# A one-layer attention block: x loaded through other queues, tiles of x and weights by turns in the first chunk, and the norm's squares from a second load of x by rows

## The chip, the cores and the metric

The kernel runs on one core of a Trainium2 chip. The metric is the device time of one execution in microseconds (us); lower is better. The engines are PE (TensorE, matrix products), ACT (ScalarE), DVE (VectorE), POOL (GpSimd) and SP (SyncE, which here only issues transfers). ACT, POOL and SP can issue transfers (DMAs) as well; each engine works through its own instructions in their order, and an instruction that waits holds up all behind it.

## The reference

The input x has 512 tokens of 4096 features. With one layer, the block is:

```
h   = x * rsqrt(mean(x*x) + eps) * norm_g          # RMS norm over the features
q, k, v, z = split(h @ w_in + b_in)                # 4096 x 9216 weights
o   = attention(q, k, v)                           # causal window of 128 keys, sinks
x   = x + (o * z * sigmoid(z)) @ w_out + b_out     # 4096 x 4096 weights
out = x * rsqrt(mean(x*x) + eps) * final_g
```

All arrays are float32.

## The kernel before

**Precision.** A float32 operand is split into a high part in PE's format and a low remainder. ACT makes the high part, DVE the low one, and each product is three matmuls: high by high, high by low, low by high.

**Input projection.** The contraction over 4096 features runs in `NC` = 8 chunks `kc` of `KC` = 4 tiles of 128 features. The columns of `w_in` form 72 tiles `t` of 128. One *slot* (kc, t) is 4 feature tiles by 3 matmuls, so 12 matmuls of 128x128 by 128x512. Weights of a slot are 256 KB; `load_w` (L151) brings them through SP's queue into one of `RAW` = 3 buffers, and `split_w` (L160) splits them into `whi` (ACT, L128) and `wlo` (DVE, L129), with `WB` = 4 buffers of each.

**The stage that matters here** comes first: while x arrives, the first `NPRE` = 4 column tiles run chunk by chunk (L492), 8 chunks by 4 slots, 32 slots in all. Later column tiles find all of x split in SBUF.

**Loading x** (`load_x`, L186). x comes transposed, feature by token. A transfer of 512 KB brings two feature tiles (`xraw`, two buffers, so one chunk); the first chunk takes four of 256 KB. All of them go through SP's queue, among the weights. Of each tile ACT makes `xh` (L199, with the norm's gain), DVE `xl` (L200). For the norm, tiles are squared (`xq`; the first four on POOL, L209, the others on ACT, L207), and POOL adds all squares up (L213). The gain's factor per token (`norm_column`, L229) follows behind slot (7, 1): PE sums the squares over the features in 8 small matmuls (`pv`), then DVE and ACT take the inverse root, and PE spreads it to a row behind slot (7, 2).

**What sets the order.** PE runs in the order of the text. A scheduler orders the other engines when the program is built; `tc.issue_after` sets an instruction behind another. Ahead of the first load lie `WARM` = 9 matmuls on zeros.

**Later work.** Attention of each group of heads runs behind later slots, its output goes to DRAM through POOL's queue (L465); then follow the output projection, residual and final norm (`scale_out`, `land`, `bring`).

Of the kernel before, what the change touches and what calls it, by code (L numbers as in the profile page):

```python
# [8 lines left out]
F32 = mybir.dt.float32  # L9
# [21 lines left out]
NCC = D // CW  # L31
EPS = 1e-5
# [9 lines left out]
def hybrid_block_kernel(  # L42
# [25 lines left out]
    # 1 where the key lies in the query's own block (key <= query); queries of two heads on the rows  # L68
# [10 lines left out]
    nc.scalar.activation(ones[:, 2:], ones[:, 2:], AF.Exp)  # L79
# [15 lines left out]
    # The tensor engine runs in the order of this text.  # L95
# [6 lines left out]
    # Work that is due behind a later slot of the projections' matmuls.  # L102
# [29 lines left out]
    def rsqrt(v, y, n):  # L132
        """y = v ** -0.5, one Newton step behind the table's root."""
        a = small.tile([P, n], F32, name="rs_a", tag="rs_a", bufs=2)
        nc.scalar.activation(a, v, AF.Sqrt)
        nc.vector.reciprocal(y, a)
        nc.vector.tensor_tensor(a, y, y, op=ALU.mult)
        nc.vector.tensor_tensor(a, a, v, op=ALU.mult)
        nc.vector.tensor_scalar(a, a, -0.5, 1.5, op0=ALU.mult, op1=ALU.add)
        nc.vector.tensor_tensor(y, y, a, op=ALU.mult)  # L140

    # Work beside the weights' stream takes its turn behind the latest of its loads and splits.
# [8 lines left out]
    def load_w(src, half=None):  # L151
        """Two tiles of weights, or one; split as they are needed."""
        raw = wpool.tile([P, 2, CW], F32, name="raw", tag="raw", bufs=RAW)
        if half is None:
            latest[0] = nc.sync.dma_start(raw, src.rearrange("p (j c) -> p j c", j=2))
        else:
            latest[0] = nc.sync.dma_start(raw[:, half], src)  # L157
        return raw
# [8 lines left out]
    with ExitStack() as ph:  # L167
# [5 lines left out]
        # the tensor engine's clock is let up by work alone: run it on zeros until the first loads land  # L173
# [10 lines left out]
        squares = [None]  # L184

        def load_x(kc, whole=True):  # L186
            xh[kc] = xg.tile([P, KC, S], F32R, name=f"xh{kc}", tag="hi", bufs=NC)
            xl[kc] = xg.tile([P, KC, S], F32R, name=f"xl{kc}", tag="lo", bufs=NC)
            for i in range(KC // 2):
                raw = att.tile([P, 2, S], F32, name="xraw", tag="q2", bufs=2)  # L190
                src = xT[kc * KC // 2 + i].rearrange("p (j s) -> p j s", j=2)
                if whole:
                    nc.sync.dma_start(raw, src)
                for j in range(2):
                    if not whole:
                        nc.sync.dma_start(raw[:, j], src[:, j])
                    kt = kc * KC + 2 * i + j
                    h, l = xh[kc][:, 2 * i + j, :], xl[kc][:, 2 * i + j, :]
                    high = nc.scalar.activation(h, raw[:, j], AF.Copy, scale=gcol[:, kt:kt + 1])  # L199
                    nc.vector.scalar_tensor_tensor(  # L200
                        l, raw[:, j], gcol[:, kt:kt + 1], h.bitcast(F32),
                        op0=ALU.mult, op1=ALU.subtract,
                    )
                    q = att.tile([P, S], F32, name="xq", tag="tmp" if kt else "z", bufs=2 if kt else 1)
                    with tc.issue_after(high.ins):
                        if whole:
                            nc.scalar.activation(q, raw[:, j], AF.Square)  # L207
                        else:
                            nc.gpsimd.tensor_tensor(q, raw[:, j], raw[:, j], op=ALU.mult)  # L209
                    if kt == 0:  # L210
                        squares[0] = q
                    else:
                        nc.gpsimd.tensor_tensor(squares[0], squares[0], q, op=ALU.add)  # L213

        def mm_chunk(acc, kc, raw):
            wh, wl = split_w(raw, kc % 2)
            for j in range(KC):
                h, l = wh[:, j * P:(j + 1) * P], wl[:, j * P:(j + 1) * P]
                xhj, xlj = xh[kc][:, j, :], xl[kc][:, j, :]
                mm(acc, h, xhj, start=(kc == 0 and j == 0), stop=False)  # L220
                mm(acc, h, xlj, start=False, stop=False)
                mm(acc, l, xhj, start=False, stop=(kc == NC - 1 and j == KC - 1))
# [6 lines left out]
        def norm_column():  # L229
            """rsqrt(mean(x[t]**2) + EPS), a block of tokens in a column."""  # L230
            pv = ps_t.tile([P, NB, 2], F32, name="pv", tag="pt")
            for b in range(NB):
                mm(pv[:, b], squares[0][:, b * P:(b + 1) * P], ones[:, 0:2], start=True, stop=True)
            v = small.tile([P, NB], F32, name="v4")
            nc.vector.tensor_scalar(v, pv[:, :, 0], 1.0 / D, EPS, op0=ALU.mult, op1=ALU.add)
            r = small.tile([P, NB], F32, name="r4")
            rsqrt(v, r, NB)
            return r

        def norm_row(r):  # L240
# [14 lines left out]
        def kv_tile(g, acc):  # L255
# [12 lines left out]
            # vv[:, m]: the values of the 128 keys from 64 (m - 1) on; vw[:, m]: those of the 64 keys  # L268
            # from 64 m on, twice
# [23 lines left out]
        def q_tile(g, p, acc):  # L293
# [12 lines left out]
            # the high parts of both pairs of a four, one above the other  # L306
# [58 lines left out]
        def turn(n, pr):  # L365
            """The weights by key, split in two: the window's first 128 keys, and the 64 that follow."""
# [40 lines left out]
        def quad(g, i, q2, qh, kh, vv, vw):  # L407
            """The attention of a group's heads 4i to 4i + 3."""
# [31 lines left out]
        def gate(g, p, acc):  # L440
            """z / (1 + exp(-z))."""
# [48 lines left out]
        NPRE = 4  # L490
        accs = [ps_m.tile([P, S], F32, name="acc") for _ in range(NPRE)]
        for kc, t in ((kc, t) for kc in range(NC) for t in range(NPRE)):  # L492
            k2, i = divmod(kc, 2)
            raw = load_w(w_in[t, k2, :, i * CW:(i + 1) * CW], half=i)
            if t == 0 == kc:
                with tc.issue_after(latest[0].ins):
                    nc.sync.dma_start(gcol, norm_g)
                    load_x(kc, False)
            if t == 1 and kc < NC - 1:
                with tc.issue_after(latest[0].ins):  # L500
                    load_x(kc + 1)
            mm_chunk(accs[t], kc, raw)
            if kc == NC - 1:
                if t == 1:
                    r = norm_column()
                elif t == 2:
                    norm_row(r)
                for i in {2: (0, 1, 2), 3: (3,)}.get(t, ()):
                    evacuate(i, accs[i])
        for t in range(NPRE, NT):  # L510
            acc = ps_m.tile([P, S], F32, name="acc")
            for kc in range(NC):
                if kc % 2 == 0:
                    raw = load_w(w_in[t, kc // 2])
                mm_chunk(acc, kc, raw)
                if t == NT - 1 and kc:
                    behind(lambda: load_g(kc - 1))
                if t == NT - 1 and kc == NC - 1:
                    evacuate(t, acc)
                tick()  # L520
# [50 lines left out]
    def scale_out(tb, fg, xb):  # L571
        """The final norm of a block's rows, a chunk of columns at a time; the last has its gains to come."""
# [37 lines left out]
    for cc in range(NCC):  # L610
# [6 lines left out]
        for kt in range(HOLD, KT) if last else ():  # L617
            # the last weights stay, so that the blocks end one after the other
# [18 lines left out]
def _columns():  # L637
    """The projection's columns by key-value head: k and v, then queries and gates, two heads at a time."""
# [45 lines left out]
```

## Time and profile before

| | |
|---|---|
| time, median of 3 runs | 2437.08 us (2435.55 to 2439.21) |
| profiled execution, its span | 2435.7 us, 1.4 us below the median; no time of its own is listed apart |
| PE busy | 2406.7 us, 99% of the span |
| DVE, ACT, POOL busy | 1436.5, 992.8, 362.2 us |
| DMA | 266.31 MB, 109 GB/s over the span |

The first of the profile's 40 slices are the stage in which x arrives: PE is busy for 8 tenths of the first slice, and 9 or more in the next ones, where matmuls at half clock count as busy too. So the busy share alone hides what is lost; the timeline, with start times of single matmuls, shows it. The granted clock (PEclk) is 1.00 at 2.4 GHz and 0.50 at 1.2 GHz.

### The profile page before, as it was taken

What the parts mean: (1) busy time and instruction counts of PE and PEld (TensorE: products, weight loads), DVE (VectorE), ACT (ScalarE), POOL (GpSimd) and SP (SyncE); (2) the same over time, 40 slices, a digit from 0 to 9 for tenths busy, and PEclk for the clock granted to TensorE, in tenths of its full rate; (3) what the DMA queues carried; (4) which work ended last, traced back from release to release, by engine and by line L of the source; (5) the groups of instructions that cost most, each with busy time, mean ns of one, the idle gap of its engine ahead of it and who ended that gap; (6) DMA issues with size and microseconds to landing.
All of it is one profiled execution on the core that took longest, in us unless ns stands there. A gap on an engine that the chain in (4) does not pass through costs nothing.

```text
span 2435.7 us, 30364 instructions
## 1 busy us (share of the span) xinstructions
PE 2406.7 (99%) x11033; PEld 1999.4 (82%) x11033; DVE 1436.5 (59%) x2513; ACT 992.8 (41%) x2142; POOL 362.2 (15%) x459
## 2 busy tenths in 40 slices
PE   8899999999999999999999999999999999999997
PEld 6688888888888888888888888888888888888886
DVE  7576465646646464564655556465765664665565
ACT  5454343333434333342433334343444444444444
POOL 6221110201111020110101011010210110110110
PEclk9999999999999999999999999999999999999999
DMA  5323323323232333223233232323733432343335
GB/s 188 124 88 95 104 91 91 102 90 102 85 104 87 100 96 96 95 91 100 91 93 101 88 102 85 103 88 102 261 117 102 127 122 95 121 123 99 125 117 182
DMA packets 80550, 266.31 MB, mean 109 GB/s; under 512 B 9440, under 2 KB 9472, under 8 KB 80400
## 3 DMA queue, kind: packets, MB, share of 16 engines
q1 hardware_dynamic: 73904, 243.32, 32.4%
q0 software_dynamic: 6496, 21.05, 2.6%
q8 instruction: 87, 1.43, 0.2%
q14 instruction: 63, 0.52, 0.1%
HBM read 247.55 MB, written 16.78 MB: 109 GB/s over the span
## 4 chain that ended last, share of the span: by engine, by line
PE 97%; DVE 1%; DMA 1%; issue 1%; ACT 0%; POOL 0%; SPq 0%; DVEq 0%; POOLq 0%
PE acc L97 92%; PE ps L97 2%; PE po L97 2%; PE pt L100 1%; DMA xraw<-in_xT 1%; DVE xl L200 0%; DVE wlo L129 0%; PE pv L100 0%; ACT xh L199 0%; DVE y L586 0%; ACT xq L207 0%; ACT whi L128 0%; POOL wl L379 0%; SPq L157 0%; POOL wh L379 0%
## 5 line engine op out<-in xcount | busy, mean ns | idle before, releaser
L129 DVE TENSOR_TENSOR wlo<-raw,whi 128x512 fp32r<-128x512 f32 x822 | 596.0, 727 | 758.7 <-ACT whi L128 749.1
L128 ACT CAST whi<-raw 128x512 fp32r<-128x512 f32 x822 | 510.9, 622 | 1208.1 <-PE acc L97 1154.0
L97 PE MATMUL acc<-xh,wlo 128*128 128x512 f32 x2304 | 901.4, 391 | 11.7 <-DVE wlo L129 11.6
L97 PE MATMUL acc<-xh,whi 128*128 128x512 f32 x2304 | 904.7, 393 | 2.4 <-ACT xh L199 1.9
L97 PE MATMUL acc<-xl,whi 128*128 128x512 f32 x2304 | 900.9, 391 | 0.6 <-DVE xl L200 0.4
L97 PE MATMUL acc<-whi,gs 128*128 128x512 f32 x1968 | 606.3, 389 | 0.0
L97 PEld LDWEIGHTS acc<-xh,wlo 128*128 128x128 f32 x2304 | 433.9, 188 | 107.4 <-DVE wlo L129 15.5
L97 PEld LDWEIGHTS acc<-xh,whi 128*128 128x128 f32 x2304 | 434.5, 189 | 89.2 <-ACT xh L199 2.8
L97 PEld LDWEIGHTS acc<-xl,whi 128*128 128x128 f32 x2304 | 434.3, 188 | 87.8 <-DVE xl L200 2.9
L97 PEld LDWEIGHTS acc<-whi,gs 128*128 128x128 f32 x1968 | 369.6, 188 | 76.4
L97 PE MATMUL acc<-wlo,gs 128*128 128x512 f32 x984 | 383.2, 389 | 0.0
L97 PEld LDWEIGHTS acc<-wlo,gs 128*128 128x128 f32 x984 | 184.8, 188 | 38.2
L129 DVE TENSOR_TENSOR gs<-g,gs 128x512 fp32r<-128x512 f32 x256 | 191.2, 788 | 0.6 <-ACT gs L128 0.6
L379 POOL TENSOR_SCALAR_AFFINE_SELECT ww<-wh 64x512 fp32r<-64x512 f32 x64 | 42.1, 658 | 830.6 <-ACT wh L375 830.6
L128 ACT CAST gs<-g 128x512 fp32r<-128x512 f32 x256 | 145.8, 617 | 1.7 <-PE acc L97 1.7
L353 ACT ACTIVATE prob<-ps,nm 128x128 f32<-128x128 f32 x256 | 90.3, 365 | 78.6 <-DVE nm L344 75.0
L451 DVE RECIPROCAL e<-e 128x128 f32<-128x128 f32 x128 | 120.7, 945 | 0.5
L598 POOL DMA_DIRECT2D xb<-in_x x32 | 17.3, 540 | 502.3 <-DVE y L608 502.3
L428 ACT COPY ot<-po 64x256 f32<-64x256 f32 x128 | 47.0, 367 | 55.6 <-DVE o L429 40.1
L429 DVE TENSOR_TENSOR o<-po,ot 64x256 f32<-64x256 f32 x128 | 52.8, 412 | 20.3 <-ACT ot L428 19.8
L302 DVE SCALAR_TENSOR_TENSOR q<-tmp,bcol,q 64x512 fp32r<-64x512 f32 x64 | 59.4, 927 | 6.6 <-ACT q L301 5.4
L226 DVE TENSOR_TENSOR tmp<-acc,rbc 128x512 f32<-128x512 f32 x41 | 28.4, 692 | 57.2 <-PE acc L97 56.7
(111 smaller groups left out, 1501.6 us busy)
## 6 DMA issues: line engine op xcount, KB each, us to landing
raw<-in_w_in SPq DMA_DIRECT2D x272, 512.0 KB, 3.6
raw<-in_w_out SPq DMA_DIRECT2D x128, 512.0 KB, 3.6
raw<-in_w_in SPq DMA_DIRECT2D x32, 256.0 KB, 3.2
gT<-o POOLq DMA_DIRECT2D x32, 256.0 KB, 2.3
g<-gT SPq DMA_DIRECT2D x16, 512.0 KB, 7.0
xb<-in_x POOLq DMA_DIRECT2D x32, 256.0 KB, 3.6
out_y<-y SPq DMA_DIRECT2D x32, 256.0 KB, 3.0
xraw<-in_xT SPq DMA_DIRECT2D x14, 512.0 KB, 4.2
```

The source lines that it names most:

```text
L97: tc.keep_in_program_order(nc.tensor.matmul(*a, **k))
L100: tc.keep_in_program_order(nc.tensor.transpose(*a, **k))
L128: nc.scalar.copy(hi, src),
L129: nc.vector.tensor_tensor(lo, src, hi.bitcast(F32), op=ALU.subtract),
L226: nc.vector.tensor_tensor(t, acc, rbc, op=ALU.mult)
L302: nc.vector.scalar_tensor_tensor(q2[other, :, h, :], tv[own], b[own], q2[own, :, h, :].bitcast(F32), op0=ALU.add, op1=ALU.subtract,)
L353: nc.scalar.activation(pr[:, u, a, :], ps[:, u, a, 0:P], AF.Exp, bias=nm[:, u, a:a + 1], scale=SCALE, accum_out=den[:, u, a:a + 1],)
L379: nc.gpsimd.affine_select(out=out, in_=src.bitcast(F32), fill=0.0, pattern=[[0, 8], [1 if own else -1, QH]], compare_op=ALU.is_ge if own e ...
L428: nc.scalar.copy(ot[own], pq[other, :, :, h, :])
L429: nc.vector.tensor_tensor(ov[own], pq[own, :, :, h, :], ot[own], op=ALU.add)
L451: nc.vector.reciprocal(c, c)
L598: nc.gpsimd.dma_start(xb, x[tb * P:(tb + 1) * P, cs])
```

## The change

1. **Queues.** The four transfers of x's first chunk are issued by ACT, the fourteen of 512 KB by POOL; SP carries weights and the gains alone. Staging takes four buffers by turns (tags `q2`, `o`, `q2`, `qq`), so two chunks.
2. **Order.** `x_tile` splits one tile of x behind the weights' split of a slot, one per slot and one chunk ahead. In chunk 0, tile m of x and weights of column tile m come by turns, and PE takes the products as both exist (3, then 9, 15 and 21 matmuls) instead of slot by slot.
3. **Squares.** `xq` and POOL's sums are gone. Instead `x_row` loads x again by rows, token by feature, in 16 pieces of 128 tokens by 1024 features (512 KB), through POOL's queue into two buffers (tags `vv`, `vw`), and ACT squares each with a sum into a column of `sums`. `norm_column` adds four columns on DVE; the 8 matmuls `pv` are gone.
4. The first ACT function (`Exp` on `ones`, with its table) is placed behind the first issues. Comments and docstrings are gone too; they are left out below.

```diff
+RC = 4
...
-        def load_x(kc, whole=True):
+        STAGE = ("q2", "o", "q2", "qq")
+        def load_x(kc):
...
             for i in range(KC // 2):
-                raw = att.tile([P, 2, S], F32, name="xraw", tag="q2", bufs=2)
-                if whole:
-                    nc.sync.dma_start(raw, src)
+                k2 = kc * KC // 2 + i
+                tag = STAGE[k2 % len(STAGE)]
+                raw = att.tile([P, 2, S], F32, name="xraw", tag=tag, bufs=2 if tag == "q2" else 1)
+                if kc:
+                    nc.gpsimd.dma_start(raw, src)
                 for j in range(2):
-                    if not whole:
-                        nc.sync.dma_start(raw[:, j], src[:, j])
...
-                    q = att.tile([P, S], F32, name="xq", tag="tmp" if kt else "z", bufs=2 if kt else 1)
-                    with tc.issue_after(high.ins):
-                        if whole:
-                            nc.scalar.activation(q, raw[:, j], AF.Square)
-                        else:
-                            nc.gpsimd.tensor_tensor(q, raw[:, j], raw[:, j], op=ALU.mult)
-                    if kt == 0:
-                        squares[0] = q
-                    else:
-                        nc.gpsimd.tensor_tensor(squares[0], squares[0], q, op=ALU.add)
+                    if not kc:
+                        nc.scalar.dma_start(raw[:, j], src[:, j])
+                    landed[2 * k2 + j] = raw[:, j]
+        def x_tile(kt):
+            kc, j = divmod(kt, KC)
+            raw = landed.pop(kt)
+            h, l = xh[kc][:, j, :], xl[kc][:, j, :]
+            high = nc.scalar.activation(h, raw, AF.Copy, scale=gcol[:, kt:kt + 1])
+            low = nc.vector.scalar_tensor_tensor(
+                l, raw, gcol[:, kt:kt + 1], h.bitcast(F32), op0=ALU.mult, op1=ALU.subtract
+            )
+            return high, low
+        def x_row(i):
+            tb, c = divmod(i, RC)
+            w = D // RC
...
+            nc.gpsimd.dma_start(raw, x[tb * P:(tb + 1) * P, c * w:(c + 1) * w])
+            nc.scalar.activation(raw, raw, AF.Square, accum_out=sums[:, tb, c:c + 1])
...
-            pv = ps_t.tile([P, NB, 2], F32, name="pv", tag="pt")
-            for b in range(NB):
-                mm(pv[:, b], squares[0][:, b * P:(b + 1) * P], ones[:, 0:2], start=True, stop=True)
-            nc.vector.tensor_scalar(v, pv[:, :, 0], 1.0 / D, EPS, op0=ALU.mult, op1=ALU.add)
+            nc.vector.tensor_reduce(v, sums, axis=AX.X, op=ALU.add)
+            nc.vector.tensor_scalar(v, v, 1.0 / D, EPS, op0=ALU.mult, op1=ALU.add)
...
+        load_x(0)
+        raws = [load_w(w_in[0, 0, :, 0:CW], half=0)]
+        nc.sync.dma_start(gcol, norm_g)
+        nc.scalar.activation(ones[:, 2:], ones[:, 2:], AF.Exp)
+        raws += [load_w(w_in[m, 0, :, 0:CW], half=0) for m in range(1, RAW)]
+        load_x(1)
+        for m in range(NPRE):
+            if m == RAW:
+                raws.append(load_w(w_in[m, 0, :, 0:CW], half=0))
+            first.append(after(last, split_w, raws[m], 0))
+            last = after(latest[1:], x_tile, m)
+            for t, j in [(m, j) for j in range(m)] + [(t, m) for t in range(m + 1)]:
+                mm_tile(accs[t], 0, j, *first[t])
+        for j in range(KC):
+            last = after(last, x_tile, KC + j)
+        for kc, t in ((kc, t) for kc in range(1, NC) for t in range(NPRE)):
...
+            w = split_w(raw, i)
+            if kc < NC - 1:
+                if t == 0:
+                    load_x(kc + 1)
+                last = after(latest[1:], x_tile, (kc + 1) * KC + t)
+            if ROW0 <= kc * NPRE + t < ROW0 + NB * RC:
+                after(latest[1:], x_row, kc * NPRE + t - ROW0)
+            mm_chunk(accs[t], kc, w)
```

Where the instructions come to stand (names: `raw` weights, `xraw` x transposed, `row` x by rows; xN is a count of equal instructions in a row):

SP's queue from the start of the program, before:

```order
L157 DMA raw<-in_w_in 128x512
L497 DMA gcol<-in_norm_g 128x32
L196 DMA xraw<-in_xT 128x512 x4
L157 DMA raw<-in_w_in 128x512 x3
L193 DMA xraw<-in_xT 128x1024
L157 DMA raw<-in_w_in 128x512 x3
L193 DMA xraw<-in_xT 128x1024
```

and from its end of the stage, before:

```order
L193 DMA xraw<-in_xT 128x1024 x2
L157 DMA raw<-in_w_in 128x512 x4
L193 DMA xraw<-in_xT 128x1024 x2
L157 DMA raw<-in_w_in 128x512 x6
```

The same queue over the whole stage, now:

```order
L157 DMA raw<-in_w_in 128x512
L516 DMA gcol<-in_norm_g 128x32
L157 DMA raw<-in_w_in 128x512 x31
```

No transfer of x stands behind a weight load any more, and none of the weights behind one of x.

ACT while the tiles of chunk 5 are split (`xh_567`), before:

```order
L199 ACTIVATE xh_567<-xraw,gcol 128x512
L128 CAST whi<-raw 128x512
L207 ACTIVATE xq<-xraw 128x512
L199 ACTIVATE xh_567<-xraw,gcol 128x512
L207 ACTIVATE xq<-xraw 128x512
L199 ACTIVATE xh_567<-xraw,gcol 128x512 x2
L128 CAST whi<-raw 128x512
L207 ACTIVATE xq<-xraw 128x512 x2
L128 CAST whi<-raw 128x512 x2
```

and now (`xh_519`):

```order
L211 ACTIVATE xh_519<-xraw,gcol 128x512
L227 ACTIVATE row,sums<-row 128x1024 x2
L128 CAST whi<-raw 128x512
L211 ACTIVATE xh_519<-xraw,gcol 128x512
L128 CAST whi<-raw 128x512
L211 ACTIVATE xh_519<-xraw,gcol 128x512
L227 ACTIVATE row,sums<-row 128x1024
L128 CAST whi<-raw 128x512
L211 ACTIVATE xh_519<-xraw,gcol 128x512
L227 ACTIVATE row,sums<-row 128x1024
```

The splits of x and of the weights now alternate, and squares of rows stand between them; a `whi` behind a square waits for that square's transfer.

POOL behind its constants, before:

```order
L209 TENSOR_TENSOR xq<-xraw 128x512 x3
L213 TENSOR_TENSOR xq<-xq 128x512 x2
L209 TENSOR_TENSOR xq<-xraw 128x512
L213 TENSOR_TENSOR xq<-xq 128x512 x29
```

and now, the first rows and the last:

```order
L200 DMA xraw<-in_xT 128x1024 x2
L226 DMA row<-in_x 128x1024 x2
L200 DMA xraw<-in_xT 128x1024 x6
L226 DMA row<-in_x 128x1024
L200 DMA xraw<-in_xT 128x1024
L226 DMA row<-in_x 128x1024
```

```order
L200 DMA xraw<-in_xT 128x1024
L226 DMA row<-in_x 128x1024
L200 DMA xraw<-in_xT 128x1024
L226 DMA row<-in_x 128x1024 x6
```

POOL computes nothing in this stage any more; it issues 14 transfers of x and 16 of rows in one order, each waiting for its buffer. Behind this stage the instructions of every engine stand in the same order as before.

## Rows read from the trace of the kernel before

**Rows 1.** The page: span, and the engines' shares of the chain that ended last.

```profile
span 2435.7 us, 30364 instructions
...
PE 97%; DVE 1%; DMA 1%; issue 1%; ACT 0%; POOL 0%; SPq 0%; DVEq 0%; POOLq 0%
```

**Rows 2.** Waits of PE from 112 us to the end: total us, times, longest.

```profile
PE po L97 <- POOL wl L379: 0.4, 1, 0.4
```

**Rows 3.** Timeline of PE: start us, us, engine, line, operation, out<-in, count, idle before.

```profile
6.17 0.51 PE L97 MATMUL acc<-xh,whi 128*128 128x512 f32 x1 [1.31 <-ACT xh L199]
...
9.90 0.63 PE L97 MATMUL acc<-xh,wlo 128*128 128x512 f32 x1
10.33 0.63 PE L97 MATMUL acc<-xh,whi 128*128 128x512 f32 x1
...
22.17 0.39 PE L97 MATMUL acc<-xh,whi 128*128 128x512 f32 x1
...
111.46 0.95 PE L97 MATMUL pv<-ones,xq 128*128 128x2 f32 x8
112.27 0.48 PE L97 MATMUL acc<-xh,whi 128*128 128x512 f32 x1
```

**Rows 4.** Stretches: bounds, length, busy us (count) by engine, PEclk, DMA share, GB/s.

```profile
22.17:42.80 20.63, 20.13 (x87) 15.77 (x85) 17.75 (x16) 15.00 (x26) 15.31 (x10) 1.00 0.65 205
42.80:111.62 68.82, 57.11 (x229) 44.33 (x229) 40.11 (x39) 29.86 (x53) 23.12 (x16) 0.95 0.46 147
```

**Rows 5.** Timeline of ACT behind the last x tile.

```profile
108.71 0.62 ACT L128 CAST whi<-raw 128x512 fp32r<-128x512 f32 x1 [2.10 <-PE acc L97]
111.43 0.62 ACT L128 CAST whi<-raw 128x512 fp32r<-128x512 f32 x1 [2.10 <-PE acc L97]
```

**Rows 6.** Waits of SP's queue from 0 to 112 us, then timelines of SP and ACT.

```profile
SPq L157 <- DVE wlo L129: 63.7, 25, 9.4
...
54.36 12.87 SPq L157 DMA_DIRECT2D raw<-in_w_in  x4
67.28 2.73 SPq L193 DMA_DIRECT2D xraw<-in_xT  x2
...
73.00 0.72 ACT L199 ACTIVATE xh<-xraw,gcol 128x512 fp32r<-128x512 f32 x1 [8.91 <-DMA xraw<-in_xT]
```

**Rows 7.** Groups and operations up to 115 us: count, ns as mean or min/median/max.

```profile
L213 POOL TENSOR_TENSOR xq<-xq 128x512 f32<-128x512 f32 x31 | 46.6, 1505 | 38.8 <-ACT xq L207 37.6
L199 ACT ACTIVATE xh<-xraw,gcol x32: 705/716/726, 5.4 to 92.6; 128x512 fp32r<-128x512 f32 x32
L200 DVE SCALAR_TENSOR_TENSOR xl<-xraw,gcol,xh x32: 739/1463/1804, 6.2 to 95.7; 128x512 fp32r<-128x512 f32 x32
L128 ACT CAST whi<-raw x34: 601/611/625, 3.7 to 111.4; 128x512 fp32r<-128x512 f32 x34
L129 DVE TENSOR_TENSOR wlo<-raw,whi x33: 676/692/1780, 4.9 to 109.4; 128x512 fp32r<-128x512 f32 x33
```

**Rows 8.** Stretches of 2 us, columns as in rows 4.

```profile
2.00:4.00 2.00, 2.00 (x6) 0.76 (x5) 0.40 (x1) 0.57 (x3) 1.82 (x6) 1.00 0.77 235
4.00:6.00 2.00, 0.86 (x4) 0.11 (x1) 0.80 (x2) 0.94 (x2) 0.74 (x2) 1.00 0.80 212
6.00:8.00 2.00, 1.25 (x3) 0.48 (x3) 0.89 (x1) 0.49 (x2) 0.82 (x2) 0.92 0.95 302
```

**Rows 9.** Squares of the last stage, DMA issues of POOL, and landing of x tiles and xb.

```profile
L606 ACT ACTIVATE y<-xb x32: 613/627/634, 1812.6 to 2423.9; 128x512 f32<-128x512 f32 x32
L606 ACT ACTIVATION_READ_ACCUMULATOR y<-xb x32: 183/186/189, 1813.1 to 2424.5; 128x1 f32 x32
...
L465 POOL DMA_DIRECT2D gT<-o x32: 547/549/584, 181.5 to 1738.6; - x32
...
DMA to landing us min/median/max: 3.5/4.3/7.1
...
DMA to landing us min/median/max: 3.1/3.6/10.9
```

More of the change, by code (lines that the diff above doesn't have):

```diff
@@ L78, in hybrid_block_kernel @@
     nc.vector.memset(ones, 1.0)
-    nc.scalar.activation(ones[:, 2:], ones[:, 2:], AF.Exp)
     gcol = const.tile([P, KT], F32, name="gcol")
@@ L182, in hybrid_block_kernel @@
         xl = [None] * NC
-        squares = [None]
-        def load_x(kc, whole=True):
+        landed = {}
+        sums = small.tile([P, NB, RC], F32, name="sums")
+        STAGE = ("q2", "o", "q2", "qq")
+        def load_x(kc):
             xh[kc] = xg.tile([P, KC, S], F32R, name=f"xh{kc}", tag="hi", bufs=NC)
@@ L189, in load_x @@
             for i in range(KC // 2):
-                raw = att.tile([P, 2, S], F32, name="xraw", tag="q2", bufs=2)
-                src = xT[kc * KC // 2 + i].rearrange("p (j s) -> p j s", j=2)
-                if whole:
-                    nc.sync.dma_start(raw, src)
-                for j in range(2):
-                    if not whole:
-                        nc.sync.dma_start(raw[:, j], src[:, j])
[L197 to L203, printed above, removed]
-                    q = att.tile([P, S], F32, name="xq", tag="tmp" if kt else "z", bufs=2 if kt else 1)
-                    with tc.issue_after(high.ins):
-                        if whole:
-                            nc.scalar.activation(q, raw[:, j], AF.Square)
-                        else:
-                            nc.gpsimd.tensor_tensor(q, raw[:, j], raw[:, j], op=ALU.mult)
-                    if kt == 0:
-                        squares[0] = q
-                    else:
-                        nc.gpsimd.tensor_tensor(squares[0], squares[0], q, op=ALU.add)
@@ L215, in mm_chunk @@
-        def mm_chunk(acc, kc, raw):
-            wh, wl = split_w(raw, kc % 2)
-            for j in range(KC):
[L218 to L222, printed above, removed]
+                k2 = kc * KC // 2 + i
@@ new lines, in load_x @@
+                tag = STAGE[k2 % len(STAGE)]
+                raw = att.tile([P, 2, S], F32, name="xraw", tag=tag, bufs=2 if tag == "q2" else 1)
+                src = xT[k2].rearrange("p (j s) -> p j s", j=2)
+                if kc:
+                    nc.gpsimd.dma_start(raw, src)
+                for j in range(2):
+                    if not kc:
[10 more added lines that the diff above has]
+            return high, low
@@ new lines, in x_row @@
+        def x_row(i):
+            tb, c = divmod(i, RC)
+            w = D // RC
+            if i % 2:
+                raw = att.tile([P, 2, S], F32, name="row", tag="vw", bufs=1).rearrange("p a s -> p (a s)")
+            else:
+                raw = att.tile([P, S // QH + 1, 2, HD], F32, name="row", tag="vv", bufs=1)
+                raw = raw.rearrange("p m a d -> p (m a d)")[:, 0:w]
+            nc.gpsimd.dma_start(raw, x[tb * P:(tb + 1) * P, c * w:(c + 1) * w])
+            nc.scalar.activation(raw, raw, AF.Square, accum_out=sums[:, tb, c:c + 1])
@@ new lines, in after, with mm_tile @@
+        def after(instructions, fn, *a):
+            with ExitStack() as turn:
+                for ins in instructions:
+                    turn.enter_context(tc.issue_after(ins.ins))
+                return fn(*a)
+        def mm_tile(acc, kc, j, wh, wl):
+            h, l = wh[:, j * P:(j + 1) * P], wl[:, j * P:(j + 1) * P]
+            xhj, xlj = xh[kc][:, j, :], xl[kc][:, j, :]
+            mm(acc, h, xhj, start=(kc == 0 and j == 0), stop=False)
+            mm(acc, h, xlj, start=False, stop=False)
+            mm(acc, l, xhj, start=False, stop=(kc == NC - 1 and j == KC - 1))
@@ L224, in scaled, with mm_chunk @@
+        def mm_chunk(acc, kc, w):
+            for j in range(KC):
+                mm_tile(acc, kc, j, *w)
         def scaled(acc, tag="tmp"):
@@ L490, in hybrid_block_kernel @@
         NPRE = 4
+        ROW0 = NPRE + 4
         accs = [ps_m.tile([P, S], F32, name="acc") for _ in range(NPRE)]
-        for kc, t in ((kc, t) for kc in range(NC) for t in range(NPRE)):
+        load_x(0)
[4 more added lines that the diff above has]
+        load_x(1)
+        first = []
+        last = ()
+        for m in range(NPRE):
[8 more added lines that the diff above has]
+        for kc, t in ((kc, t) for kc in range(1, NC) for t in range(NPRE)):
             k2, i = divmod(kc, 2)
             raw = load_w(w_in[t, k2, :, i * CW:(i + 1) * CW], half=i)
[L495 to L500, printed above, removed]
+            w = split_w(raw, i)
+            if kc < NC - 1:
+                if t == 0:
                     load_x(kc + 1)
-            mm_chunk(accs[t], kc, raw)
+                last = after(latest[1:], x_tile, (kc + 1) * KC + t)
+            if ROW0 <= kc * NPRE + t < ROW0 + NB * RC:
+                after(latest[1:], x_row, kc * NPRE + t - ROW0)
+            mm_chunk(accs[t], kc, w)
             if kc == NC - 1:
@@ L514, in hybrid_block_kernel @@
                     raw = load_w(w_in[t, kc // 2])
-                mm_chunk(acc, kc, raw)
+                mm_chunk(acc, kc, split_w(raw, kc % 2))
                 if t == NT - 1 and kc:
```

## The prediction, made before the changed kernel was run

> **What bounds the kernel now.** I read the chain of waits first: PE is 97% of it [rows 1], so a change counts only where PE loses time. The waits of PE come next. From 112 us to the end it waits 0.4 us in all [rows 2], and behind the first stage every engine keeps its order. So the whole question is the stage in which x arrives, from PE's first product at 6.17 us to the small matmuls `pv` at 111.46 us [rows 3].
>
> What should this stage take? Behind the last x tile ACT waits for PE before each split, and starts 2.72 us apart [rows 5]: that is PE's own pace for a slot of 12 matmuls, 0.227 us each. Thirty slots lie ahead of `pv`: 30 x 2.72 = 81.6 us. The timeline of PE has 105.3 us there, so 23.7 us are lost. Chunk 0 (6.17 to 22.17) takes 16.0 us for 10.9, a loss of 5.1. The 26 slots behind it take 89.3 us for 70.7, a loss of 18.6. Up to 42.80 us the record holds 87 matmuls in 20.63 us, which is nearly full pace; from there to 111.62 PE is busy for 57.11 of 68.82 us, with the clock at 0.95 [rows 4]. The late chunks lose almost all.
>
> SP's queue shows why. It waits 63.7 us for DVE's `wlo`, which frees weight buffers, and the transfers of the next x chunk stand behind those waits: issued at 67.28 us, only when four weight loads are away, and ACT, idle for 8.91 us, gets the tile at 73.00 [rows 6]. Then a whole chunk of x must be split at once, ahead of weights that PE needs. And DVE is slow at it: `xl` takes 739 ns at best but 1463 in the median, while POOL sums squares for 1505 ns a tile [rows 7]. Both fall in the same time; the trace doesn't part them.
>
> **The change, part by part.**
>
> *pv.* The 8 matmuls go: 112.27 - 111.46 = 0.8 us gained [rows 3]. The inverse root now starts from ACT's last square, which stands behind slot (6, 3), so three slots (8.2 us) cover it; without them it would cost PE its length.
>
> *Chunk 0.* Product m now needs x tile m and weights m, from two queues. Before, the first product at 6.17 followed an `xh` of 0.72 us [rows 3, 7], so the second transfer of 0.26 MB was there at 5.4. By rows 8 DMA had moved 0.47 MB at 4 us and 0.89 at 6, so 0.52 MB at 4.2: data are ready 1.2 us after they moved. Now the first pair (0.52 MB) is ready at 5.4 and the second (1.05 MB) at 7.7. From about 6 us POOL's transfers take a third of the engines, which leaves 201 of 302 GB/s [rows 8], 2.6 us a pair: 10.3 and 12.9. With `whi` and `xh` on ACT, 0.61 + 0.72 [rows 7], the products open at 6.7, 9.0, 11.6 and 14.2 us. At 9.90 us matmuls start 0.43 us apart, the 1.2 GHz level, after PE had idled for want of data [rows 3]; I keep that level to 14.2 us. The 9 matmuls of m = 1 end at 12.9, the 15 of m = 2 at 16.9 (three slow, twelve at 0.227), the 21 of m = 3 at 21.7. Gain: 22.17 - 21.7 = 0.5 us. At full clock from 9.0 on it would be 19.8 us (gain 2.4); with the last pair 2.8 us later, the span from the median to the longest landing of x (4.3 to 7.1 [rows 9]), and the low clock as much longer, 23.1 (loss 0.9).
>
> *ACT's four issues* show in no row. The nearest, POOL's, take 0.55 us [rows 9]; four are 2.2 us and, with the table load behind them, still end before 5.4 us. Between nothing and that I cost them at nothing; the wait for the first data covers them.
>
> *DVE.* POOL's arithmetic goes, so `xl` and `wlo` return to 0.74 + 0.69 us a slot [rows 7], 1.4 of 2.72. If `xl` stayed at its median of 1.46, 2.2 us would still fit.
>
> *ACT.* A slot costs 0.61 + 0.72 = 1.33 us. A square of 128x1024 isn't in the trace; it lies between one of 512 with its sum (0.63 + 0.19 = 0.81) and two of them (1.63) [rows 9]. I take 2 x 0.627 + 0.186 = 1.44, near the upper end because the length doubles. Over slots (2, 0) to (6, 3): 20 x 1.33 + 16 x 1.44 = 49.6 us of PE's 54.4; with 1.63 it is 52.7. It fits, with little room.
>
> *x ahead of need.* Four staging buffers and a queue without weights put x up to two chunks ahead, which PE's pace needs only one by one. POOL's issue of `gT` beside DVE's work takes 547 to 584 ns over 32 of them [rows 9], so POOL's 30 issues need 30 x 0.55 = 16.5 us of the stage. A rule speaks against moving x to POOL: the Trainium skill (SBUF — State Buffer, SBUF: two separate sides) warns that DVE copies in a two-port mode keep GpSimd from writing the descriptors of its own DMAs, 620 ns becoming 3100; by it the 30 would take an estimated 93 us. The row doesn't bear that out, and I go by the row; what a held issue would do is part of rival A.
>
> *DMA.* The second load of x adds 8.4 MB. The densest stretch is slots (2, 0) to (4, 3), 32.6 us: weights 3.15 MB, x 3.15, nine rows 4.7, together 11.0 MB. The traffic of 22.17 to 42.80 us gives 205 GB/s at a share of 0.65, so 315 at full share [rows 4]: 34.9 us, 2.3 late. At 4 to 6 us it was 212 at 0.80 [rows 8], so 265: 41.5 us, 8.9 late. Lead of x and the four split buffers may hide all. I take a new loss of 2.3, between 0 and 8.9.
>
> **Sum.** 0.5 + 0.8 + (18.6 - 2.3) = 17.6 us. On the profiled execution 2435.7 - 17.6 = 2418.1; the median of the runs stands 1.4 us above its span: 2419.5 us. Best: 2.4 + 0.8 + 18.6 = 21.8 us gained, 2415.3. Worst: -0.9 + 0.8 + 9.7 = 9.6, 2427.5. The three runs spread by some 1.8 us to either side, so 2413.5 to 2429.3.
>
> **Rivals.**
>
> *Rows late (A).* ACT works in order: a square that waits holds `whi` behind it. Two row buffers alternate, so a row is issued only after the square two before. Each buffer serves 8 rows, 7 turns in 18 slots (49 us), 7.0 us a turn. A turn is 1.44 of square, 0.55 of issue and the landing. x tiles of 512 KB landed in 4.3 us in the median [rows 9]: 6.3, in time. At their longest, 7.1, a turn is 9.1 and the seven are 14.7 late: in place of 2.3, that leaves 5.2 gained, 2431.9, at the edge of no change. An issue on POOL held for one DVE operation (1.46 [rows 7]) makes the turn 7.75, 5.3 late, 2422.5, still in the forecast's range. By the Trainium skill's 3100 ns (same page and section) the turn would be an estimated 8.8, and the time 2429.8.
>
> *Rows much too late, slower than before (B).* The same place, with POOL's queue as slow as its slowest `xb`, 10.9 us [rows 9]: turns of 12.9, 41.3 us late against 19.9 gained, so 21.4 slower: 2458.5. It becomes slower once a turn passes 7.0 + 19.9 / 7 = 9.8 us, a landing over 7.8. For it: that 10.9 stands in POOL's queue, with several transfers under way, as here. Against: the median there is 3.6.
>
> *x no sooner (C).* PE's late waits could be DMA's share of the engines, not order: then other queues bring nothing, the 18.6 us stay, and 0.5 + 0.8 leaves 2435.8. Against: the DMA share from 42.80 to 111.62 us is 0.46 [rows 4], and SP waits for DVE. The Trainium skill (DMA: Bandwidth & Descriptors, Issuing engines are not separate DMA queues) states this rule: all issuers run on the same 16 engines, and issuing from several saves only issue time. The trace bears out the shared engines, but not that order in a queue is free.
>
> **Chances.** Forecast 0.82, A 0.07, B 0.05, C 0.06. Faster means by over 0.2% (4.9 us, about what a measurement here can tell from no change), below 2432.2: the forecast and about half of A, 0.86. Same: the rest of A, and C, 0.09. Slower: B, 0.05. The range takes the forecast's bounds and the spread of the runs, 2413.5 to 2429.5, and leaves out A to C, 0.18.
>
> **What would show it.** Right: the first matmul behind slot (7, 1) starts at 92 to 97 us instead of 112.27 (22.17 - 0.5 + 70.7 + 2.3 = 94.7); chunk 1 starts near 21.7; `xl` near 0.75 us each; ACT waits for `row` and x transfers, PE little for `wlo`. Wrong: ACT's `whi` late behind `row`, with landings over 7 us (A, B); POOL issues over 1 us (A's held issue); or waits of ACT for `xraw` of 9 us as before (C).

## The result, and the profile after

The changed kernel takes **2414.86 us** (median of 4 runs, 2414.50 to 2414.99), the kernel before beside it 2436.68 (4 runs, 2435.55 to 2439.21). The ratio is 0.9909, 95% interval 0.9897 to 0.9921: 0.9% faster, 21.8 us. The profiled spans, of one execution each, are 2412.5 and 2435.7 us, 23.2 apart; runs of the kernel before alone spread over 3.7 us.

The page of the changed kernel, span and shares of the chain, answers to [rows 1]: PE had 97% and now has 99%.

```profile
span 2412.5 us, 30330 instructions
...
PE 99%; DVE 0%; DMA 0%; POOL 0%; issue 0%; ACT 0%; DVEq 0%; POOLq 0%
```

Waits of PE up to 112 us (total us, times, longest), first in the kernel before from 23 us on, where chunk 0 is over:

```profile
PE acc L97 <- DVE wlo L129: 11.6, 7, 2.7
PE acc L97 <- ACT whi L128: 0.5, 1, 0.5
```

The same view of the changed kernel, over the whole stage:

```profile
PE acc L97 <- ACT xh L211: 1.8, 1, 1.8
PE idle L97 <- DVE zero L175: 1.3, 1, 1.3
PE acc L97 <- DVE xl L212: 0.7, 1, 0.7
```

All three stand ahead of 8 us. Twelve microseconds of waits behind chunk 0 have become none. DVE's timeline in the kernel before shows one of those waits from the other side:

```profile
76.14 5.15 DVE L200 SCALAR_TENSOR_TENSOR xl<-xraw,gcol,xh 128x512 fp32r<-128x512 f32 x3
81.22 1.88 DVE L129 TENSOR_TENSOR wlo<-raw,whi 128x512 fp32r<-128x512 f32 x3
```

Three splits of x in a row, at 1.72 us each, stand ahead of the split of a weight tile for which PE waits 2.66 us, up to 81.95. At 0.75 us each they would have taken about 2.9 us less, more than the whole wait.

The timeline of PE in the changed kernel answers to [rows 3]:

```profile
6.70 0.50 PE L97 MATMUL acc<-xh,whi 128*128 128x512 f32 x1 [1.84 <-ACT xh L211]
7.94 0.80 PE L97 MATMUL acc<-xl,whi 128*128 128x512 f32 x1 [0.73 <-DVE xl L212]
8.53 0.63 PE L97 MATMUL acc<-xh,wlo 128*128 128x512 f32 x1
8.96 0.63 PE L97 MATMUL acc<-xh,whi 128*128 128x512 f32 x1
...
10.66 0.60 PE L97 MATMUL acc<-xl,whi 128*128 128x512 f32 x1
11.09 0.41 PE L97 MATMUL acc<-xh,wlo 128*128 128x512 f32 x1
11.34 0.40 PE L97 MATMUL acc<-xh,whi 128*128 128x512 f32 x1
...
20.21 0.39 PE L97 MATMUL acc<-xh,whi 128*128 128x512 f32 x1
...
90.93 0.39 PE L97 MATMUL acc<-xh,whi 128*128 128x512 f32 x1
93.66 0.61 PE L97 MATMUL pr<-ident,rb 128*128 128x128 f32 x4
```

Chunk 1 starts at 20.21 us (22.17 before), slot (7, 2) at 90.93 (112.27 before). Between these lie 26 slots: 70.72 / 26 = 2.72 us, PE's own pace, nothing lost. So 21.3 us of the spans' 23.2 come from this stage. The rest lies far behind it: the last `xb` comes 22.2 us earlier (2400.96 against 2423.20), so 0.9 between slot (7, 2) and there, and 1.0 more behind it. The first part goes with the old squares: from the first `pr` to PE's last matmul, the kernel before and the three kernels below that sum squares on POOL take 2307.6 us, the changed kernel and its other variants 2306.8 (the one with rows loaded twice, 2309.0). The second part, from the start of PE's last matmul to the end, has no such pattern: 13.0 us before, 12.0 in the changed kernel, 12.0 to 12.9 in the others. What makes either is not shown.

Groups of the changed kernel up to 115 us (count, ns as min/median/max, first and last start), and landings, answer to [rows 7, 9]:

```profile
L226 POOL DMA_DIRECT2D row<-in_x x16: 527/527/535, 5.0 to 76.5; - x16
L227 ACT ACTIVATE row<-row x16: 1042/1061/1062, 27.7 to 81.7; 128x1024 f32<-128x1024 f32 x16
L227 ACT ACTIVATION_READ_ACCUMULATOR row<-row x16: 182/184/187, 28.6 to 82.7; 128x1 f32 x16
...
DMA to landing us min/median/max: 3.9/6.1/10.5
L200 POOL DMA_DIRECT2D xraw<-in_xT x14: 527/527/550, 4.0 to 58.5; - x14
L203 ACTq DMA_DIRECT2D xraw<-in_xT x4: 407/454/457, 0.8 to 2.2; - x4
...
L212 DVE SCALAR_TENSOR_TENSOR xl<-xraw,gcol,xh x32: 744/751/754, 7.1 to 80.7; 128x512 fp32r<-128x512 f32 x32
L129 DVE TENSOR_TENSOR wlo<-raw,whi x41: 623/692/695, 6.5 to 114.5; 128x512 fp32r<-128x512 f32 x41
```

`xl` is back at 751 ns in the median, 754 at most (1463 and 1804 before). The landing of 3.9/6.1/10.5 is that of the rows.

Stretches of the changed kernel, columns as in [rows 4]: a piece of chunk 0, all slots behind it up to (7, 2), and the densest three chunks.

```profile
10.00:12.00 2.00, 2.00 (x8) 1.58 (x7) 1.46 (x3) 0.88 (x2) 0.36 (x1) 0.72 1.03 416
...
20.21:90.93 70.72, 70.72 (x313) 58.59 (x312) 35.31 (x61) 47.08 (x84) 11.78 (x23) 1.00 0.83 280
31.09:63.73 32.64, 32.64 (x145) 27.04 (x144) 14.94 (x22) 21.00 (x37) 7.27 (x14) 1.00 0.95 330
```

Behind PE, DMA is the busiest resource now, with a share of 0.95 over 32.6 us, and PE still loses nothing there.

### The profile page after: what moved, and what is told of

Same layout as the page of the kernel before. It is cut to its first block, busy times and chain, and to the rows that moved or that the text cites. A ratio compares the mean times of both kernels' runs of the same rounds, so it can differ in the third digit from the quotient of the medians.

```text
span 2412.5 us, 30330 instructions
## 1 busy us (share of the span) xinstructions
PE 2396.6 (99%) x11025; PEld 1997.2 (83%) x11025; DVE 1404.3 (58%) x2514; ACT 994.0 (41%) x2146; POOL 326.1 (14%) x454
## 4 chain that ended last, share of the span: by engine, by line
PE 99%; DVE 0%; DMA 0%; POOL 0%; issue 0%; ACT 0%; DVEq 0%; POOLq 0%
PE acc L97 94%; PE ps L97 2%; PE po L97 2%; PE pt L100 1%; DMA bcol<-in_b_in 0%; PE pv L100 0%; DVE y L625 0%; POOL wl L399 0%; POOL wh L399 0%; PE pr L97 0%; DVE xl L212 0%; ACT y L645 0%; DVE xb L644 0%; DVE y L621 0%; POOL ww L399 0%
## 5 line engine op out<-in xcount | busy, mean ns | idle before, releaser
L129 DVE TENSOR_TENSOR wlo<-raw,whi 128x512 fp32r<-128x512 f32 x822 | 582.0, 709 | 787.7 <-ACT whi L128 777.9
```

The costliest lines, as they stand in the source:

```text
L129: nc.vector.tensor_tensor(lo, src, hi.bitcast(F32), op=ALU.subtract),
```

## The experiments

My theory behind the result was that PE's late waits had two sources, which the change removes together: DVE slowed by POOL's sums, and a chunk of x split at once behind late loads. The rivals: one of the two alone; the queue; the lead that four staging buffers give. Each ratio is to the kernel before, run beside it on the same chip (2436.56, 2437.41 or 2437.04 us). The changed kernel itself, unedited, was run once more in one of these comparisons:

> The changed kernel itself, on the chip of these runs, to stand beside e8_again: 2414 to 2416 us.

Measured: 2415.00 us (2414.68 to 2415.85), ratio 0.9910 (0.9896 to 0.9923). In its trace chunk 1 starts at 20.70 us, where the first trace has 20.21, and PE again loses nothing from there to slot (7, 2). So chunk 0 of one and the same kernel moves by half a microsecond, and differences of less than about a microsecond between kernels say nothing here.

**Rows alone.** The kernel before, with the norm's squares from rows:

```diff
+            nc.gpsimd.dma_start(raw, x[tb * P:(tb + 1) * P, c * w:(c + 1) * w])
+            nc.scalar.activation(raw, raw, AF.Square, accum_out=sums[:, tb, c:c + 1])
...
-                            nc.scalar.activation(q, raw[:, j], AF.Square)
...
-                        nc.gpsimd.tensor_tensor(squares[0], squares[0], q, op=ALU.add)
```

> The kernel before with the third part of the change alone: squares from a second load of x by rows through POOL's queue, no arithmetic on POOL; x stays in SP's queue and in the old order. Theory S (POOL's sums slow DVE, and everything late follows from that): xl back to 0.75 us, the 18.6 us lost behind chunk 0 mostly come back, 2418 to 2424 us. Theory O (x stands behind weight loads in one queue and is split a whole chunk at a time): the loss stays, 2430 to 2437 us.

Measured: 2419.79 us, ratio 0.9929 (0.9917 to 0.9942). Groups of DVE, waits of PE from 23 us on, and the starts of chunks 1 and 7 on PE:

```profile
L212 DVE SCALAR_TENSOR_TENSOR xl<-xraw,gcol,xh x32: 744/751/755, 6.4 to 84.8; 128x512 fp32r<-128x512 f32 x32
...
PE acc L98 <- ACT whi L129: 1.1, 2, 0.7
PE acc L98 <- DVE wlo L130: 1.0, 1, 1.0
...
21.90 0.39 PE L98 MATMUL acc<-xh,whi 128*128 128x512 f32 x1
...
91.39 0.39 PE L98 MATMUL acc<-xh,whi 128*128 128x512 f32 x1
```

With DVE at its own pace, x still split a chunk at a time behind SP's queue costs PE little: chunk 1 starts at 21.90 and chunk 7 at 91.39, 69.49 us for 65.28 (24 slots of 2.72). Of the 18.6 us, 14.4 are gone and 4.2 stay. This edit does more than quicken DVE: ACT's squares of x and all of POOL's arithmetic go with it, and squares of rows come. No run slows or quickens DVE's splits alone; that they are what counts is argued from PE's waits, of which 11.6 of 12.1 us before were for DVE's `wlo`, and from the timeline of DVE above.

**Turns alone, three ways.** The changed kernel, with the squares as before: ACT squares the staged tile, POOL sums, `pv` is back.

```diff
-                    nc.gpsimd.dma_start(raw, src)
+                    nc.sync.dma_start(raw, src)
...
+                if kc:
+                    nc.scalar.activation(q, raw, AF.Square)
...
+                nc.gpsimd.tensor_tensor(squares[0], squares[0], q, op=ALU.add)
...
-                after(latest[1:], x_row, kc * NPRE + t - ROW0)
```

First with x on SP's queue, as in this diff:

> The changed kernel with the squares as before (ACT squares, POOL adds, 8 matmuls pv) and x's later chunks on SP's queue, in the new order with four staging buffers. Theory S: DVE slow again (xl near 1.4 us), PE waits for wlo again, 2427 to 2437 us. Theory O: x comes ahead of need in the new order, and DVE's slowness fits in a slot (2.2 of 2.72 us), 2415 to 2420 us.

Then the same without the diff's first two lines, so x on POOL's queue among the sums:

> The changed kernel with the squares as before (ACT's square, POOL's add, the product at the end), and x still issued from POOL's queue, now behind POOL's adds. If the order of x and weights and the buffers decide, and not who issues, it is like e2s: 2420 to 2423 us. If the adds hold the issues of x back (1.5 us each on POOL, and each waits for ACT's square), x comes later than in e2s and PE waits for xl: 2423 to 2437 us.

And with x on SP and two staging buffers in place of four:

```diff
-        STAGE = ("q2", "o", "q2", "qq")
+        STAGE = ("q2",)
```

> The kernel of e2s (squares from x's own load on ACT, adds on POOL and their product as before; x and weights by turns on SP's queue) with two staging buffers for x in place of four, as the kernel before has. e2s lost only 0.9 us behind chunk 0 although DVE's splits were as slow as before (xl 737/1164/1786 ns). If the turns of x and weights are what kept PE fed, this is like e2s: 2420 to 2423 us, chunks 10.88 us apart. If it was the lead that four buffers give x, PE waits again for xl and wlo in some chunks: 2425 to 2437 us, chunks 11 to 13 us apart.

Measured: 2421.35 us (ratio 0.9938, 0.9926 to 0.9951), 2419.51 (0.9927, 0.9915 to 0.9940) and 2423.05 (0.9942, 0.9930 to 0.9955). Groups of the first, `xl` on DVE and POOL's sums (count, us in all, mean ns, idle before), and PE's starts of chunks 1 and 7 in the second:

```profile
L212 DVE SCALAR_TENSOR_TENSOR xl<-xraw,gcol,xh x32: 737/1164/1786, 8.6 to 80.2; 128x512 fp32r<-128x512 f32 x32
...
L224 POOL TENSOR_TENSOR xq<-xq 128x512 f32<-128x512 f32 x31 | 48.4, 1560 | 22.7 <-ACT xq L218 21.8
...
22.70 0.39 PE L97 MATMUL acc<-xh,whi 128*128 128x512 f32 x1
...
89.12 0.39 PE L97 MATMUL acc<-xh,whi 128*128 128x512 f32 x1
```

PE's timeline of the third, its idle times from chunk 1 on:

```profile
24.98 0.50 PE L97 MATMUL acc<-xh,whi 128*128 128x512 f32 x1 [2.66 <-ACT whi L128]
25.95 0.50 PE L97 MATMUL acc<-xh,wlo 128*128 128x512 f32 x1 [0.23 <-DVE wlo L129]
29.35 0.50 PE L97 MATMUL acc<-xh,wlo 128*128 128x512 f32 x1 [0.38 <-DVE wlo L129]
```

From the start of chunk 1 to that of chunk 7 the first loses 0.9 us (23.64 to 89.80), the second 1.1 (22.70 to 89.12), the third 1.6 (24.98 to 91.84), in place of 18.6, and most of it ahead of 30 us. Yet DVE still has slow splits: of the 32 `xl`, 19 took over 1 us before; 16, 15 and 11 do in these three. So the order of the work is enough by itself: x split one tile a slot, a chunk ahead. Neither the queue nor four buffers is needed for most of the gain. Two buffers in place of four cost 1.7 us here (the third against the first), with one wait of 2.66 us where chunk 1 starts: ACT stands idle for a tile of x for 4.02 us, and the `whi` behind it starts only at 24.33. The expected cost of a held issue on POOL did not come: the second is the best of the three.

Most of what these three lose to the changed kernel, they lose at the start: chunk 1 starts 2.5 to 4.8 us later, `pv` costs 0.8, and the rest is the 0.9 to 1.6 above and what stands behind the stage. The timelines of DVE and POOL in the first show the start:

```profile
8.57 1.57 DVE L212 SCALAR_TENSOR_TENSOR xl<-xraw,gcol,xh 128x512 fp32r<-128x512 f32 x1
10.06 1.76 DVE L129 TENSOR_TENSOR wlo<-raw,whi 128x512 fp32r<-128x512 f32 x1
11.75 1.76 DVE L212 SCALAR_TENSOR_TENSOR xl<-xraw,gcol,xh 128x512 fp32r<-128x512 f32 x1
```

```profile
8.55 1.04 POOL L220 TENSOR_TENSOR xq<-xraw 128x512 f32<-128x512 f32 x1 [0.46 <-DMA xraw<-in_xT]
9.55 3.41 POOL L224 TENSOR_TENSOR xq<-xq 128x512 f32<-128x512 f32 x2
```

Beside POOL's sums a split takes 1.76 us, POOL's sum 1.70, one of each in the same time; in the changed kernel, with no arithmetic on POOL, the splits take 0.75 and 0.69. The first `xl` comes late, and PE waits 2.35 us for it at 10.20. The Trainium skill (SBUF — State Buffer, SBUF: two separate sides) has a DVE operation with two inputs in SBUF and a GpSimd one that reads SBUF exclude each other for a whole instruction; these rows agree with that.

**The queue alone.** The changed kernel with x on SP among the weights, the first two lines of the diff above and no more:

> The changed kernel with x's later chunks issued by SP instead of POOL; order, staging and rows unchanged. If the queue itself matters (x held behind weights that wait for buffers): PE waits again, 2420 to 2432 us. If only the order and the staging matter: no change, 2413 to 2417 us; rows may land sooner, since POOL then carries them alone.

Measured: 2415.81 us, ratio 0.9914 (0.9901 to 0.9928), within 1 us of the changed kernel. PE waits for nothing behind 8.01 us. Waits of SP's queue in this kernel, from 20 to 95 us:

```profile
SPq L157 <- DVE wlo L129: 41.8, 24, 4.1
```

Before, the same row read 63.7 us over the whole stage, 9.4 at the longest [rows 6], and 55.9 from 20 us on. Most of the waits are still there, and x still stands behind them, but by one transfer for two weight tiles and a chunk ahead; PE does not feel it. Moving x to POOL is worth about 1 us at most, no more than such comparisons can tell. The Trainium skill's rule (DMA: Bandwidth & Descriptors, Issuing engines are not separate DMA queues), that further issuers save only issue time, fits this result.

**PE slot by slot in chunk 0:**

```diff
-            for t, j in [(m, j) for j in range(m)] + [(t, m) for t in range(m + 1)]:
-                mm_tile(accs[t], 0, j, *first[t])
+        for t in range(NPRE):
+            mm_chunk(accs[t], 0, first[t])
```

> The changed kernel with PE's products of chunk 0 slot by slot as before, loads and splits of tiles by turns as now. The first slot then needs x tile 3, whose split ends near 15.6 us, and 36 matmuls (8.2 us) follow: chunk 1 starts near 23.9 instead of 20.2 us, so 3.7 us slower, 2418.5 us. Rival: lead of the splits gives it back later, 2415 us.

Measured: 2420.49 us, ratio 0.9935 (0.9922 to 0.9949), 5.6 us over the changed kernel, where I had expected 3.7; chunk 1 starts 5.6 us later, at 25.84, and none of it is given back behind it. Stretches of this kernel, columns as in [rows 4]:

```profile
10.00:14.00 4.00, 3.50 (x6) 1.29 (x5) 1.67 (x4) 1.41 (x3) 0.53 (x1) 0.50 1.03 410
14.00:18.00 4.00, 2.87 (x6) 1.99 (x7) 3.52 (x6) 4.00 (x7) 1.05 (x2) 0.50 1.03 374
```

and the same of the changed kernel:

```profile
10.00:14.00 4.00, 4.00 (x17) 3.22 (x16) 1.46 (x3) 1.24 (x3) 0.36 (x1) 0.86 1.03 411
14.00:18.00 4.00, 4.00 (x20) 3.30 (x19) 3.70 (x6) 3.35 (x6) 1.05 (x2) 1.00 1.06 368
```

Data come at the same rate in both. Slot by slot, PE waits for the next tile of x (0.19 us at 11.68, 1.36 at 15.13), the granted clock stays at 0.50, and the record holds 12 matmuls in these 8 us in place of 37. PE's recorded waits in chunk 0 are 1.8 us longer than in the changed kernel (4.3 against 2.5); the other 3.8 us of the loss go with the longer stay at 1.2 GHz, which I had left out of the expectation.

**No rows at all.** The sums are set to a constant and the second load is left out, so this kernel lacks the norm's factor:

```diff
+        nc.vector.memset(sums, D / RC)
...
-                after(latest[1:], x_row, kc * NPRE + t - ROW0)
```

> The changed kernel without the second load of x and its squares: the sums are set to a constant, so the norm's factor is left out. It tells what the rows cost. PE had no wait behind 7.94 us in the changed kernel, so taking the rows away should gain nothing there; only chunk 0 has 1 MB less beside its first loads, its last pair lands sooner: 2413.5 to 2415 us. Rival (the rows cost DMA or ACT time that reaches PE): 2 us or more faster, below 2413 us.

Measured: 2414.55 us, ratio 0.9908 (0.9893 to 0.9923). PE loses nothing between chunk 1 and slot (7, 2) here either. The rows, 8.4 MB and 16 squares, cost PE nothing in those slots, and in the whole time nothing that can be told from zero: the medians differ by 0.3 us, while chunk 1 starts at 21.55 in this trace.

**Rows loaded twice.** Rival B's overload, made on purpose:

```diff
             nc.gpsimd.dma_start(raw, x[tb * P:(tb + 1) * P, c * w:(c + 1) * w])
+            nc.gpsimd.dma_start(raw, x[tb * P:(tb + 1) * P, c * w:(c + 1) * w])
```

> The changed kernel with each piece of x by rows loaded twice, one transfer behind the other into the same buffer. A buffer's turn becomes square 1.24 + 2 x (issue 0.53 + landing 5 to 6) = 12.3 to 14.3 us instead of 7.25; seven turns are then 35 to 49 us longer, less a lead of some 2 us: 2448 to 2462 us, slower than the kernel before. This is the mechanism of rivals A and B at a known place beyond its turning point of 9.8 us a turn. Rival (lead of the splits and the scheduler's order hide it): 2415 to 2425 us.

Measured: 2449.96 us, ratio 1.0050 (1.0033 to 1.0067): slower than before. PE's waits up to 135 us, the groups of the rows' squares, and PE's timeline:

```profile
PE pr L97 <- DVE rb L266: 33.3, 1, 33.3
...
L228 ACT ACTIVATE row<-row x16: 1042/1056/1062, 31.7 to 123.7; 128x1024 f32<-128x1024 f32 x16
...
127.78 2.04 PE L97 MATMUL pr<-ident,rb 128*128 128x128 f32 x8 [33.34 <-DVE rb L266]
```

A buffer's turn was (123.7 - 31.7) x 2 / 15 = 12.3 us. B's sum with this turn gives the right direction and somewhat too much: (12.3 - 7.0) x 7 = 37 late against 19.9 gained makes 17 slower, measured 12 to 13. The wait of 33.3 us against the 21.8 gained without it leaves 11.5 of that. The place is another: PE lost 0.15 us from chunk 1 to slot (7, 2). The scheduler had put the last squares behind the `whi` of the stage's slots, and the wait came in one piece at the norm's row `pr`. So no run shows a `whi` behind a late square holding up PE, which was the way that A and B had named; a `whi` behind a late tile of x did so with two staging buffers.

**A better version?** Two tries on the first microseconds: the load of the fourth weight tile earlier and the rows' loads behind x's, then the same with 13 matmuls on zeros ahead (`WARM`).

```diff
+            with tc.issue_after(issued[5 + i % 2].ins):
+                nc.gpsimd.dma_start(raw, x[tb * P:(tb + 1) * P, c * w:(c + 1) * w])
...
+        latest[0] = nc.sync.dma_start(raws[0][:, 1], w_in[RAW, 0, :, 0:CW])
```

> The changed kernel with the fourth weight tile of chunk 0 loaded into the free half of the first buffer (not behind the first split), and the first two row pieces issued behind x's third chunk. The last pair of chunk 0 should be split near 12 us instead of 14.9, and PE, not data, then sets the end of chunk 0: chunk 1 starts 0.3 to 1.2 us sooner, 2413.7 to 2414.6 us. Rival: rows that start later end later and eat the lead at slot (7, 0): slower than 2415 us.

```diff
-WARM = 9
+WARM = 13
```

> The same with 13 instead of 9 matmuls on zeros ahead of the first load. If the low clock between 8 and 11 us comes from PE idling 1.8 us before its first product, PE runs at 0.227 us a matmul from the start: up to 1 us better than without, 2412.8 to 2414 us. Rival: the extra matmuls end behind the first data and delay the first product, or change nothing: 2414 to 2416 us.

The second once more, beside the changed kernel on one chip:

> e8_warm once more (row 3 of the weights earlier, rows of x later, more products ahead of the first real one), beside the changed kernel on the same chip. If its 1.1 us are real, it stands 0.7 to 1.5 us below a2_changed_again, near 2413.7; if they were the difference of two chips, within 0.5 us of it.

Measured: 2415.49 us (ratio 0.9911, 0.9897 to 0.9926), 2413.71 (0.9904, 0.9890 to 0.9919), and again 2415.51 (0.9909, 0.9896 to 0.9923) beside 2415.00 for the changed kernel. The 1.1 us of the first comparison did not return: no gain. In this stage there is nothing left to win behind chunk 0, and in chunk 0 these edits move nothing that stands out from the spread: chunk 1 starts at 20.62, 20.52 and 20.71 in the three traces, at 20.21 and 20.70 in the two of the changed kernel.

## Why the prediction was right, and where its terms were off

Forecast 2419.5 us, measured 2414.86: inside the range and the likeliest case, but 4.6 us faster than the forecast and 0.4 faster than the prediction's own best case of 2415.3. Only the 1.8 us added for the spread of the runs keep it in the range, and that is some luck: the sum put the time behind this stage at nothing, and the spans differ there by 1.9 us. (The range's upper end stands once as 2429.3 and once as 2429.5; 2427.5 + 1.8 is the first.) The terms, in us gained:

| term | predicted | measured in the trace |
|---|---|---|
| chunk 0 | 0.5 (-0.9 to 2.4) | 2.0 (22.17 to 20.21) |
| `pv` | 0.8 | 0.8 |
| behind chunk 0 | 18.6 - 2.3 | 18.6 - 0.0 |
| elsewhere | 0 | 1.9 |
| sum, on the spans | 17.6 | 23.2 (rounded terms: 23.3); 21.8 on the medians |

- *What bounds the kernel*: right as to the place. All of the gain that I can explain is PE's lost time in this stage, and slot (7, 2) came at 90.93, earlier than my 92 to 97. As to the cause, "SP's queue shows why" was half right: x on that queue behind those waits does no harm once it goes tile by tile a chunk ahead. The sentence behind it, "Then a whole chunk of x must be split at once, ahead of weights that PE needs. And DVE is slow at it", names what the runs bore out.
- *Chunk 0*: the opening times were right, the clock was not. I had the products of the first two pairs open at 6.7 and 9.0 us; they started at 6.70 and 8.96, the second held by PE's own earlier products, since its `xh` was done at 8.75. The step that failed is "I keep that level to 14.2 us": from 11.09 us on matmuls start 0.23 to 0.25 us apart, the 2.4 GHz level. From 8.96 to 11.09 PE worked without a gap at 1.2 GHz. I had twelve matmuls at 0.43 us from 9.0 us on, and five came; seven at 0.23 in place of 0.43 us are 1.4 us, which is the miss.
- *The new loss of 2.3*: 0. The rate per share was taken too low. Over 31.09 to 63.73 us DMA moved 330 GB/s at a share of 0.95, by the same scaling 347 at full share against my 315 and 265; at 10 to 12 us it moved 416. What lateness was left was hidden, as I had allowed: `whi` of slot (2, 0) started 4.6 us ahead of its slot (26.52 against 31.09), that of (7, 0) 2.7 us ahead (82.79 against 85.49). So 1.9 us of lead were used up, and PE did not see it.
- *ACT's square*: 1.06 + 0.18 = 1.24 us, not 1.44; inside my bounds of 0.81 and 1.63.
- *ACT's four issues*: 1.86 us in all from 0.81 us on, and the first split starts at 5.41 with the weights' landing. Nothing, as predicted.
- *DVE*: right, 0.75 + 0.69 us a slot. But the late chunks do not need it once x goes by turns: there they run nearly at pace beside slow splits. On top of the turns, POOL's absence is worth 4.5 us (2419.51 against 2415.00, x on POOL's queue in both): about 2 in chunk 0, 0.8 for `pv`, 1.1 in chunk 1, the rest behind the stage.
- *POOL's issues*: 527 to 550 ns, none held, beside DVE's splits. The Trainium skill's 3100 ns (SBUF — State Buffer, SBUF: two separate sides), given there for a transfer beside a DVE copy in a two-port mode, did not show beside these splits of two inputs.
- *Rival A*: the rows' landing rose to 6.1 us in the median and 10.5 at most, more than the 4.3 of my forecast and less than A's 7.1 for each. A turn of the even buffer was 7.25 us (squares from 27.65 to 78.39, 7 turns) for the 7.0 that hide it: 1.7 late in all, about the lead that was used up.
- *Rival B*: did not happen. The doubled rows show that rows far too late make the kernel slower than before, but at `pr` and not by way of a held `whi`.
- *Rival C*: refuted, since the 18.6 us went while DMA's share rose from 0.46 to 0.83 and more. Its other half, that the queue itself brings nothing, is true.

What the trace of before could not part, x's order and the squares on POOL that slow DVE, the runs do. Medians, in us:

| | x a chunk at once | x by turns |
|---|---|---|
| squares summed on POOL | 2436.6 | 2419.5 to 2423.1 |
| squares from rows | 2419.8 | 2414.9 |

The two gains, 16.8 and 14.0 to 17.5, do not add up, since the late chunks' loss can be removed once only: most of it needed the squares on POOL and x at once together.

## What to carry to other kernels

When an engine waits behind two causes that strike at the same time, removing either may return most of the loss; run each alone before a complicated change is credited to all its parts. Look at the order in which the work of several engines interleaves before its queue and its buffers: here the order was worth 14 to 17.5 us, the queue about 1. A transfer may be added almost free if its consumer has lead to spare. Where it stops being free can be estimated from a buffer's turn, that is square, issue and landing against the slots it serves; the one test of that sum here, at a turn of 12.3 us, gave 17 us slower where 12.5 were measured.

## What was not expected of the hardware

- PE's waits cost more here than their length. Before, PE idled 12.1 us behind chunk 0 and lost 18.6. A stretch of the kernel before, from 80 to 90 us, shows a part of the difference, a mean granted clock of 0.83: after the wait of 2.66 us that ends at 81.95, PE's matmuls start 0.43 us apart from 83.15 to 86.14, the 1.2 GHz level, and after one of 2.11 us that ends at 51.32 from 52.17 to 55.15 (columns as in [rows 4]):

```profile
80.00:90.00 10.00, 8.05 (x28) 6.50 (x29) 3.15 (x5) 0.80 (x2) 0.75 (x1) 0.83 0.60 178
```

- With the rows, x and the weights under way, DMA moved 330 GB/s over 32.6 us at a share of 0.95, while PE, ACT and DVE worked at their usual durations (matmuls 389 ns, `xh` 720, `xl` 751); from 10 to 12 us it moved 416.
- The landing of x's tiles grew from 4.3 to 6.1 us in the median, and PE lost nothing by it, with ACT waiting 12.0 us for rows and 15.8 for weights in the meantime.
